# Both halves of a split input as one moving operand, and a reciprocal in pieces

## The chip, the cores and the metric

The kernel runs on one core of a Trainium2 chip. The metric is the device time of one execution in microseconds (us). TensorE multiplies 128x128 weight tiles (the stationary operand) with a moving operand of 256 or 512 columns here, into banks of PSUM (128x512 fp32 each); VectorE (DVE), ScalarE (ACT) and GpSimd (POOL) do the rest, and each works off its own queue of instructions in order. SyncE (SP) issues most of the DMAs.

## The reference

One layer of a streaming encoder over 256 frames of 2048 features. Four mixers share one input projection, each has a gate as wide as the model, and a SwiGLU block follows:

```python
h = rms_norm(x, norm_mix_pre[l])
z = h @ w_in[l]
z_conv, z_gla, z_diff, z_rwkv, z_gate = jnp.split(z, _offsets(TOP_SIZES), axis=-1)
...
merged = gates[:, :, 0] * (o_conv @ w_branch[l, 0])
...
# gla: log_a = log_sigmoid(w_lr @ w_a2 + b_a) / GLA_LOGIT_NORM
```

The sum over the four gated branches goes through `w_out`, a second norm and a residual, and then through gate, up and down projections of 5632 features. All products are wanted at fp32 accuracy. In the linear attention (gla), a log-sigmoid of the decay is computed with a series that needs one reciprocal of a 128x512 tile.

## The kernel before, in words

**Split products.** fp32 accuracy is built from operands rounded to fp32r. Each operand is held as a rounded half (`hi`) and the remainder (`lo`), and a product is three matmuls: hi x hi, hi x lo and lo x hi. The weights come from memory in chunks of 256 rows by 512 columns (512 KB). `Stream.chunk` loads a chunk on SP's queue, rounds it on ScalarE (the cast, L600) and takes the remainder on VectorE (the subtraction, L601); it has four buffers for raw chunks and three for each of hi and lo. The normalised input is split the same way into `hT_hi` and `hT_lo` (L361 and L362, in `split_out`), 16 k-tiles of 128 features by 256 frames.

**Two kinds of product.** A token-major product (`gemm_tok`, L661 to L663) has the input as weights and 512 weight columns as the moving operand; it takes two banks, one for each 128 frames. A feature-major product (`gemm_feat`, L692, L693, L695) has the weights as stationary operand and the 256 frames as the moving one: for each k-tile and each of four column tiles, three matmuls of 256 columns. Its four results of 128x256 lie in two banks, two to a bank. The first of them (`w_l`, called l) computes its lo x hi part one chunk later (`trail`, L679), since its weights and x arrive together at the start. `x_piece` brings x in five pieces meanwhile, and `x_norm` computes the norm.

**Order of the stages.** There are ten feature-major products: l, k, r and v of the RWKV mixer one behind the other, then c1, c2 and c0 of the conv mixer, later one for q and k of the linear attention, and two for q and k of the differential attention (`dq`, twice). Between and behind them stand token-major products: gates and branch products (`gates_and_branch`), values, `w_out`, and the feed-forward block. All use one pool of four banks (`bank()`, tag mm), handed out in turn, so a product of two banks leaves the other two to be read meanwhile.

**What reads the banks.** After a feature-major product, VectorE reads each bank once, multiplying by the norm `rB`: L857 to L859 for l, L863 for k, r, v, L878 and L882 in conv, L906 and L907, L933. In the conv mixer, L572 reads c0's banks directly.

**What sets the order.** Every instruction is placed on its engine's queue by a scheduler that plays the program through with its own estimate of times and takes, among the instructions that are ready, the one of the highest priority; on the chip each queue then runs in that fixed order. `tc.high_priority(offset=e.boost)` is the priority of the chunk stream, `e.mix` (lower) that of the RWKV mixer, whose small fp32 matmuls are threaded between the large ones. The linear attention's reciprocal is L421, in `gla_mixer`.

**Places.** `gt_tile` is a ring of three buffers, for the gates, the conv mixer's ct and cu, and at the start a table. The skew (SKEW = 320 bytes) shifts where hi and lo begin in their buffers for feature-major products.

Of the kernel before, what the change touches and what calls it, by code (L numbers as in the profile page):

```python
# [13 lines left out]
SKEW = 320  # L14
# [387 lines left out]
def gla_mixer(e, q, k, wl, v, g, wa2, out_hi, out_lo):  # L402
# [18 lines left out]
    V.reciprocal(h, h)  # L421
# [160 lines left out]
class Stream:  # L582
# [5 lines left out]
    def chunk(self, ap, w=512, into=None, skew=0):  # L588

        e, nc = self.e, self.e.nc  # L590
        with e.tc.high_priority(offset=e.boost):
            raw = self.ring.tile([128, 2, 512], F32, tag="raw", name="raw", bufs=e.nraw)
            nc.sync.dma_start(raw[:, :, :w], ap)
            if into:
                hi, lo = into
            else:
                o = skew // 4
                hi, lo = (self.ring.tile([128, 1152], F32R, tag=t, name=t, bufs=e.nhi)[:, o:o + 1024].rearrange("p (k n) -> p k n", k=2)
                          for t in ("hi", "lo"))
# [5 lines left out]
def hybrid_kernel(tc, x, xt, w_l, w_in, w_branch, w_out, w_gate, w_up, w_down, post_mix, post_ffn, wa2_d, w2_d, a2_d, g2_d, lq_d,  # L605
# [4 lines left out]
    e = Env()  # L610
# [4 lines left out]
    with ExitStack() as ctx:  # L615
# [8 lines left out]
        def bank():  # L624
            return mmp.tile([128, 512], F32, tag="mm", name="mm", bufs=4)
# [40 lines left out]
        def columns(w, g):  # L666
            return lambda kc: w[kc, g]

        def gemm_feat(src, w, tiles, banks, before=None, trail=False):

            held = []

            def remainder(kc, lo):
                for k in range(2):
                    kt = 2 * kc + k
                    for j, (o, wd) in enumerate(tiles):
                        mm(banks[j // 2][:wd, (j % 2) * 256:(j % 2) * 256 + 256], lo[:, k, o:o + wd], hT_hi[:, kt, :], start=False,  # L679
                           stop=kt == 15, skip_group_check=True)  # L680

            for kc in range(8):
                if before:
                    before(kc)
                hi, lo = stream.chunk(src(kc), w, skew=SKEW)
                for k in range(2):
                    kt = 2 * kc + k
                    for j, (o, wd) in enumerate(tiles):
                        ps = banks[j // 2][:wd, (j % 2) * 256:(j % 2) * 256 + 256]
                        first, last = kt == 0 and j % 2 == 0, kt == 15  # L690
                        cs = slice(o, o + wd)
                        mm(ps, hi[:, k, cs], hT_hi[:, kt, :], start=first, stop=False, skip_group_check=True)  # L692
                        mm(ps, hi[:, k, cs], hT_lo[:, kt, :], start=False, stop=False, skip_group_check=True)  # L693
                        if not trail:
                            mm(ps, lo[:, k, cs], hT_hi[:, kt, :], start=False, stop=last, skip_group_check=True)  # L695
                if trail:
                    if held:
                        remainder(*held.pop())
                    held.append((kc, lo))
            if held:  # L700
                remainder(*held.pop())
# [5 lines left out]
        hT_hi = hpool.tile([128, 16, 256], F32R, tag="hT_hi", name="hT_hi")  # L707
        hT_lo = hpool.tile([128, 16, 256], F32R, tag="hT_lo", name="hT_lo")
# [48 lines left out]
        with ExitStack() as mctx:  # L757
# [49 lines left out]
            two = lambda b: b.rearrange("p (f t) -> p f t", f=2)  # L807
# [4 lines left out]
            with ExitStack() as rctx:  # L812
# [33 lines left out]
                for q, c0 in (("l", None), ("k", COL["rk"]), ("r", COL["rr"]), ("v", COL["rv"])):  # L846
# [3 lines left out]
                    bk = [bank(), bank()]  # L850
                    if q == "l":
                        gemm_feat(lambda kc: w_l[kc], 464,
                                  [(0, 112), (112, 96), (208, 128), (336, 128)], bk, before=first_x, trail=True)
# [3 lines left out]
                        V.tensor_tensor(z[:96, 0:2, 1:257], two(bk[0])[:96], rb2(rB, slice(0, 96)), op=ALU.mult)  # L857
                        V.tensor_tensor(glw[96:112], bk[0][96:112, 0:256], rB[96:112], op=ALU.mult)
                        V.tensor_tensor(z[:, 2:4, 1:257], two(bk[1]), rb2(rB), op=ALU.mult)  # L859
                    else:  # L860
                        gemm_feat(columns(w_in, c0), 512, [(128 * j, 128) for j in range(4)], bk, before=then_tables(q))
                        for p in range(2):
                            V.tensor_tensor(z[:, 2 * p:2 * p + 2, 1:257], two(bk[p]), rb2(rB), op=ALU.mult)  # L863
# [10 lines left out]
                bk = [bank(), bank()]  # L874
                ctiles = [(128 * j, 128) for j in range(4)]
                gemm_feat(columns(w_in, COL["c1"]), 512, ctiles, bk)
                for p in range(2):
                    V.tensor_tensor(ct[:, 2 * p:2 * p + 2], two(bk[p]), rb2(rB2), op=ALU.mult)  # L878
                bk = [bank(), bank()]
                gemm_feat(columns(w_in, COL["c2"]), 512, ctiles, bk)  # L880
                for p in range(2):
                    V.tensor_tensor(cu[:, 2 * p:2 * p + 2, 2:258], ct[:, 2 * p:2 * p + 2], two(bk[p]), op=ALU.mult)  # L882
                bk = [bank(), bank()]
                gemm_feat(columns(w_in, COL["c0"]), 512, ctiles, bk)
                conv_mixer(e, cu, [two(b) for b in bk], rB, ct, *oT)
# [10 lines left out]
            with ExitStack() as sctx:  # L896
# [7 lines left out]
                bk = [bank(), bank()]  # L904
                gemm_feat(columns(w_in, COL["gqk"]), 512, ctiles, bk)
                V.scalar_tensor_tensor(q, two(bk[0]), 0.125, rb2(rB), op0=ALU.mult, op1=ALU.mult)  # L906
# [291 lines left out]
```

## Time and profile before

| | |
|---|---|
| median of 3 runs | 1647.31 us (1645.69 to 1647.57) |
| the profiled execution's own time | 1645.97 us |
| its span, first to last instruction | 1644.2 us |
| instructions | 21813, of which 8632 matmuls |
| read from HBM | 302.40 MB, 186 GB/s over the span |

The profile is of one execution. The span is shorter than the time of the execution by what lies around it. A matmul's busy time (281 ns for 256 columns, 390 for 512) overlaps the next one's, so a mean duration is not the pace at which they follow each other; the distance of two starts is. PEld is the loading of weights, which runs beside the matmuls.

### The profile page before, as it was taken

The numbers are of one execution on the slowest core, as the hardware profiler recorded it, in microseconds if no ns is written. First come the engines' busy times: TensorE is split into PE (matmuls) and PEld (weight loads), VectorE is DVE, ScalarE is ACT, GpSimd is POOL, SyncE is SP. The second block draws the span as 40 slices with busy tenths as digits, with TensorE's granted clock in tenths as the row PEclk, the third lists the DMA queues.
The fourth block names the chain that finished last, engine by engine and source line by source line (L and its number), as shares of the span: only waits on it lengthen the run. The fifth ranks groups of instructions, "written<-read, shape, count | busy, mean of one in ns | idle before, by whom it ended". The sixth has DMA issues, their size and how long they took to land.

```text
span 1644.2 us, 21813 instructions
## 1 busy us (share of the span) xinstructions
PE 1630.3 (99%) x8632; PEld 1384.2 (84%) x8632; DVE 994.8 (61%) x1176; ACT 759.6 (46%) x879; POOL 33.1 (2%) x46
## 2 busy tenths in 40 slices
PE   9999999999999999999999999999999999999997
PEld 9999988887789978888888888888888888888886
DVE  7568784669764477455655655444544555556555
ACT  6353443346554355444444644444444444445443
POOL 0000110000000001000000000000000000000000
PEclk9999999999999999999999999999999999999999
DMA  8554565345556545765555565555555555555563
GB/s 297 181 168 149 180 213 178 130 143 165 171 164 196 187 158 184 269 192 184 190 192 196 191 191 190 186 189 191 191 187 189 188 193 191 190 194 191 193 194 139
DMA packets 86118, 306.84 MB, mean 187 GB/s; under 512 B 9600, under 2 KB 12176, under 8 KB 85504
## 3 DMA queue, kind: packets, MB, share of 16 engines
q1 hardware_dynamic: 84352, 298.85, 55.6%
q0 software_dynamic: 1232, 5.95, 1.2%
q8 instruction: 67, 1.10, 0.3%
q10 hardware_dynamic: 432, 0.66, 0.2%
q14 instruction: 35, 0.29, 0.1%
HBM read 302.40 MB, written 3.01 MB: 186 GB/s over the span
## 4 chain that ended last, share of the span: by engine, by line
PE 97%; issue 1%; ACT 1%; DVE 1%; DMA 0%; POOL 0%; DVEq 0%; POOLq 0%; ACTq 0%
PE mm L662 22%; PE mm L663 21%; PE mm L661 21%; PE mm L692 5%; PE mm L693 4%; PE mm L695 4%; PE mm L1075 2%; PE mm L1077 2%; PE mm L1076 2%; PE wd L1077 2%; PE wd L1076 2%; PE wd L1075 2%; PE tq L1053 1%; PE mm L679 0%; PE ps L465 0%
## 5 line engine op out<-in xcount | busy, mean ns | idle before, releaser
L601 DVE TENSOR_TENSOR lo<-raw,hi 128x1024 fp32r<-128x1024 f32 (+1 forms) x554 | 676.6, 1222 | 550.9 <-ACT hi L600 548.7
L600 ACT CAST hi<-raw 128x1024 fp32r<-128x1024 f32 (+1 forms) x554 | 582.4, 1051 | 721.4 <-PE mm L663 510.1
L662 PE MATMUL mm<-lo,h_hi 128*128 128x512 f32 x704 | 274.9, 390 | 0.0
L663 PE MATMUL mm<-hi,h_lo 128*128 128x512 f32 x704 | 273.9, 390 | 0.1
L661 PE MATMUL mm<-hi,h_hi 128*128 128x512 f32 x704 | 250.6, 391 | 0.2 <-ACT h_hi L361 0.2
L662 PE MATMUL mm<-lo,hT_hi 128*128 128x512 f32 x608 | 238.8, 393 | 2.3 <-DVE lo L601 2.3
L663 PE MATMUL mm<-hi,hT_lo 128*128 128x512 f32 x608 | 237.5, 391 | 0.0
L661 PE MATMUL mm<-hi,hT_hi 128*128 128x512 f32 x608 | 219.5, 391 | 0.0
L692 PE MATMUL mm<-hT_hi,hi 128*128 128x256 f32 (+2 forms) x640 | 178.8, 284 | 0.3 <-ACT hi L600 0.3
L693 PE MATMUL mm<-hT_lo,hi 128*128 128x256 f32 (+2 forms) x640 | 177.1, 281 | 0.3 <-DVE hT_lo L362 0.3
L695 PE MATMUL mm<-hT_hi,lo 128*128 128x256 f32 x576 | 161.6, 282 | 0.0
L661 PEld LDWEIGHTS mm<-hi,h_hi 128*128 128x128 f32 x704 | 132.2, 188 | 27.8 <-ACT h_hi L361 0.9
L663 PEld LDWEIGHTS mm<-hi,h_lo 128*128 128x128 f32 x704 | 132.2, 188 | 27.6 <-DVE s L643 0.5
L662 PEld LDWEIGHTS mm<-lo,h_hi 128*128 128x128 f32 x704 | 132.2, 188 | 27.0
L662 PEld LDWEIGHTS mm<-lo,hT_hi 128*128 128x128 f32 x608 | 114.2, 188 | 27.2 <-DVE lo L601 2.7
L661 PEld LDWEIGHTS mm<-hi,hT_hi 128*128 128x128 f32 x608 | 114.1, 188 | 24.1
L663 PEld LDWEIGHTS mm<-hi,hT_lo 128*128 128x128 f32 x608 | 114.2, 188 | 23.6 <-issue 0.3
L692 PEld LDWEIGHTS mm<-hT_hi,hi 128*128 128x128 f32 (+2 forms) x640 | 119.8, 187 | 2.1 <-ACT hi L600 0.8
L693 PEld LDWEIGHTS mm<-hT_lo,hi 128*128 128x128 f32 (+2 forms) x640 | 120.1, 188 | 1.4 <-DVE hT_lo L362 0.5
L695 PEld LDWEIGHTS mm<-hT_hi,lo 128*128 128x128 f32 x576 | 108.7, 189 | 0.6
L1077 PE MATMUL mm<-hi,al 128*128 128x512 f32 x168 | 65.4, 389 | 0.0
L1076 PE MATMUL mm<-lo,ah 128*128 128x512 f32 x168 | 65.4, 389 | 0.0
(367 smaller groups left out, 1688.3 us busy)
## 6 DMA issues: line engine op xcount, KB each, us to landing
raw<-in_w_in_dram SPq DMA_DIRECT2D x224, 512.0 KB, 3.5
raw<-in_w_gate_dram SPq DMA_DIRECT2D x88, 512.0 KB, 3.5
raw<-in_w_up_dram SPq DMA_DIRECT2D x88, 512.0 KB, 3.5
raw<-in_w_down_dram SPq DMA_DIRECT2D x88, 512.0 KB, 3.5
raw<-in_w_branch_dram SPq DMA_DIRECT2D x32, 512.0 KB, 4.0
raw<-in_w_out_dram SPq DMA_DIRECT2D x32, 512.0 KB, 3.5
raw<-in_w_l_dram SPq DMA_DIRECT2D x8, 464.0 KB, 7.3
xs<-in_x_dram POOLq DMA_DIRECT2D x1, 2048.0 KB, 12.2
```

Source lines behind the costliest of these rows:

```text
L600: nc.scalar.copy(hi[:, :, :w], raw[:, :, :w])
L601: nc.vector.tensor_tensor(lo[:, :, :w], raw[:, :, :w], hi[:, :, :w].bitcast(F32), op=ALU.subtract)
L661: mm(banks[i_], ah[:, ts], hi[:, k, :], start=kt == 0, stop=False)
L662: mm(banks[i_], ah[:, ts], lo[:, k, :], start=False, stop=False)
L663: mm(banks[i_], al[:, ts], hi[:, k, :], start=False, stop=kt == nk - 1)
L692: mm(ps, hi[:, k, cs], hT_hi[:, kt, :], start=first, stop=False, skip_group_check=True)
L693: mm(ps, hi[:, k, cs], hT_lo[:, kt, :], start=False, stop=False, skip_group_check=True)
L695: mm(ps, lo[:, k, cs], hT_hi[:, kt, :], start=False, stop=last, skip_group_check=True)
L1053: T.transpose(ps[:, k, i * 128:(i + 1) * 128], sg[:, i, (2 * kp + k) * 128:(2 * kp + k + 1) * 128], ident)
L1075: mm(bk[j][i], ah[:, k, ts], hi[:, k, :], start=kt == 0, stop=False)
L1076: mm(bk[j][i], ah[:, k, ts], lo[:, k, :], start=False, stop=False)
L1077: mm(bk[j][i], al[:, k, ts], hi[:, k, :], start=False, stop=kt == 43)
```

## The change

The two halves of the input are laid side by side in one tile `hT`, per k-tile 256 columns of hi and 256 of lo, so that hi-weights x both is one matmul of 512 columns into a whole bank; lo-weights x hi, 256 columns, adds onto the first half of the bank. Each column tile has a bank of its own, so a feature-major product takes all four. At its end, `take` copies the bank's second half to the destination on ScalarE and adds the first half to it on VectorE, both at the stream's priority; the multiplication by the norm follows as a separate step in SBUF. In the first and the last chunk of a product the column tiles are computed one behind the other, in other chunks k-tile by k-tile. The skew is 0 for hi and 64 bytes for lo. The conv mixer has a further buffer `cb` from the ring. The reciprocal is four of 128x128. The tiles that later take hT's place (`h2`, `wl`) become one tile each.

```diff
     V.tensor_scalar(h, x, 2.0, None, op0=ALU.add)
-    V.reciprocal(h, h)
+    for j in range(2):
+        for p in range(2):
+
+            V.reciprocal(h[:, j, p * 128:(p + 1) * 128], h[:, j, p * 128:(p + 1) * 128])
     V.tensor_tensor(x, x, h, op=ALU.mult)
...
-                o = skew // 4
-                hi, lo = (self.ring.tile([128, 1152], F32R, tag=t, name=t, bufs=e.nhi)[:, o:o + 1024].rearrange("p (k n) -> p k n", k=2)
-                          for t in ("hi", "lo"))
+                hi, lo = (self.ring.tile([128, 1152], F32R, tag=t, name=t, bufs=e.nhi)[:, o // 4:o // 4 + 1024].rearrange("p (k n) -> p k n", k=2)
+                          for t, o in zip(("hi", "lo"), skew))
...
-        def gemm_feat(src, w, tiles, banks, before=None, trail=False):
+        def gemm_feat(src, w, tiles, before=None, trail=False):
+
 
 
 
             held = []
-
-            def remainder(kc, lo):
-                for k in range(2):
-                    kt = 2 * kc + k
-                    for j, (o, wd) in enumerate(tiles):
-                        mm(banks[j // 2][:wd, (j % 2) * 256:(j % 2) * 256 + 256], lo[:, k, o:o + wd], hT_hi[:, kt, :], start=False,
-                           stop=kt == 15, skip_group_check=True)
+            bk = [bank() for _ in tiles]
+
+            def rounded(kc, hi, k, j):
+                o, wd = tiles[j]
+                mm(bk[j][:wd], hi[:, k, o:o + wd], hT[:, 2 * kc + k].rearrange("p a t -> p (a t)"), start=kc == k == 0, stop=False,
+                   skip_group_check=True)
+
+            def remainder(kc, lo, k, j):
+                o, wd = tiles[j]
+                mm(bk[j][:wd, 0:256], lo[:, k, o:o + wd], hT_hi[:, 2 * kc + k, :], start=False, stop=kc == 7 and k == 1,
+                   skip_group_check=True)
+
+            def order(kc):
+                kj = [(k, j) for k in range(2) for j in range(len(tiles))]
+
+                return sorted(kj, key=lambda x: x[1]) if kc in (0, 7) else kj
 
             for kc in range(8):
                 if before:
                     before(kc)
-                hi, lo = stream.chunk(src(kc), w, skew=SKEW)
-                for k in range(2):
-                    kt = 2 * kc + k
-                    for j, (o, wd) in enumerate(tiles):
-                        ps = banks[j // 2][:wd, (j % 2) * 256:(j % 2) * 256 + 256]
-                        first, last = kt == 0 and j % 2 == 0, kt == 15
-                        cs = slice(o, o + wd)
-                        mm(ps, hi[:, k, cs], hT_hi[:, kt, :], start=first, stop=False, skip_group_check=True)
-                        mm(ps, hi[:, k, cs], hT_lo[:, kt, :], start=False, stop=False, skip_group_check=True)
-                        if not trail:
-                            mm(ps, lo[:, k, cs], hT_hi[:, kt, :], start=False, stop=last, skip_group_check=True)
+                hi, lo = stream.chunk(src(kc), w, skew=(0, 64))
+                for k, j in order(kc):
+                    rounded(kc, hi, k, j)
+                    if not trail:
+                        remainder(kc, lo, k, j)
                 if trail:
-                    if held:
-                        remainder(*held.pop())
                     held.append((kc, lo))
-            if held:
-                remainder(*held.pop())
+                    for c, l in held if kc == 7 else held[:-1]:
+                        for k, j in order(c):
+                            remainder(c, l, k, j)
+                    held = held[-1:]
+
+            def take(dst, j, r=slice(0, 128)):
+                with tc.high_priority(offset=e.boost):
+                    S.copy(dst, bk[j][r, 256:512])
+                    V.tensor_tensor(dst, dst, bk[j][r, 0:256], op=ALU.add)
+            return take
 
         def lhs_h(kt):
             return hT_hi[:, kt, :], hT_lo[:, kt, :]
 
 
-        hT_hi = hpool.tile([128, 16, 256], F32R, tag="hT_hi", name="hT_hi")
-        hT_lo = hpool.tile([128, 16, 256], F32R, tag="hT_lo", name="hT_lo")
+        hT = hpool.tile([128, 16, 2, 256], F32R, tag="hT", name="hT")
+        hT_hi, hT_lo = hT[:, :, 0], hT[:, :, 1]
...
                     if q == "l":
-                        gemm_feat(lambda kc: w_l[kc], 464,
-                                  [(0, 112), (112, 96), (208, 128), (336, 128)], bk, before=first_x, trail=True)
+                        take = gemm_feat(lambda kc: w_l[kc], 464,
+                                         [(0, 112), (112, 96), (208, 128), (336, 128)], before=first_x, trail=True)
+                        for j in range(4):
+                            p = slice(0, 96 if j < 2 else 128)
+                            take(z[p, j, 1:257], j, p)
+                            if j == 0:
+                                take(glw[96:112], 0, slice(96, 112))
                         x_norm()
                         o = VCOL["w0"][0]
                         V.tensor_scalar(half, vec[:, o:o + 8], 0.5, None, op0=ALU.mult)
-                        V.tensor_tensor(z[:96, 0:2, 1:257], two(bk[0])[:96], rb2(rB, slice(0, 96)), op=ALU.mult)
-                        V.tensor_tensor(glw[96:112], bk[0][96:112, 0:256], rB[96:112], op=ALU.mult)
-                        V.tensor_tensor(z[:, 2:4, 1:257], two(bk[1]), rb2(rB), op=ALU.mult)
+                        V.tensor_tensor(z[:96, 0:2, 1:257], z[:96, 0:2, 1:257], rb2(rB, slice(0, 96)), op=ALU.mult)
+                        V.tensor_tensor(glw[96:112], glw[96:112], rB[96:112], op=ALU.mult)
+                        V.tensor_tensor(z[:, 2:4, 1:257], z[:, 2:4, 1:257], rb2(rB), op=ALU.mult)
                     else:
-                        gemm_feat(columns(w_in, c0), 512, [(128 * j, 128) for j in range(4)], bk, before=then_tables(q))
-                        for p in range(2):
-                            V.tensor_tensor(z[:, 2 * p:2 * p + 2, 1:257], two(bk[p]), rb2(rB), op=ALU.mult)
+                        take = gemm_feat(columns(w_in, c0), 512, ctiles, before=then_tables(q))
+                        for j in range(4):
+                            take(z[:, j, 1:257], j)
+                        V.tensor_tensor(z[:, :, 1:257], z[:, :, 1:257], rb4(rB), op=ALU.mult)
...
-                bk = [bank(), bank()]
-                ctiles = [(128 * j, 128) for j in range(4)]
-                gemm_feat(columns(w_in, COL["c1"]), 512, ctiles, bk)
-                for p in range(2):
-                    V.tensor_tensor(ct[:, 2 * p:2 * p + 2], two(bk[p]), rb2(rB2), op=ALU.mult)
-                bk = [bank(), bank()]
-                gemm_feat(columns(w_in, COL["c2"]), 512, ctiles, bk)
-                for p in range(2):
-                    V.tensor_tensor(cu[:, 2 * p:2 * p + 2, 2:258], ct[:, 2 * p:2 * p + 2], two(bk[p]), op=ALU.mult)
-                bk = [bank(), bank()]
-                gemm_feat(columns(w_in, COL["c0"]), 512, ctiles, bk)
-                conv_mixer(e, cu, [two(b) for b in bk], rB, ct, *oT)
+                cb = gt_tile()[:, 0:1024].rearrange("p (f t) -> p f t", f=4)
+                take = gemm_feat(columns(w_in, COL["c1"]), 512, ctiles)
+                for j in range(4):
+                    take(ct[:, j], j)
+                V.tensor_tensor(ct, ct, rb4(rB2), op=ALU.mult)
+                take = gemm_feat(columns(w_in, COL["c2"]), 512, ctiles)
+                for j in range(4):
+                    take(cu[:, j, 2:258], j)
+                V.tensor_tensor(cu[:, :, 2:258], cu[:, :, 2:258], ct, op=ALU.mult)
+                take = gemm_feat(columns(w_in, COL["c0"]), 512, ctiles)
+                for j in range(4):
+                    take(cb[:, j], j)
+                conv_mixer(e, cu, [cb[:, 0:2], cb[:, 2:4]], rB, ct, *oT)
...
-                bk = [bank(), bank()]
-                gemm_feat(columns(w_in, COL["gqk"]), 512, ctiles, bk)
-                V.scalar_tensor_tensor(q, two(bk[0]), 0.125, rb2(rB), op0=ALU.mult, op1=ALU.mult)
-                V.tensor_tensor(k, two(bk[1]), rb2(rB), op=ALU.mult)
+                take = gemm_feat(columns(w_in, COL["gqk"]), 512, ctiles)
+                for j in range(4):
+                    take((q, k)[j // 2][:, j % 2], j)
+                V.scalar_tensor_tensor(q, q, 0.125, rb2(rB), op0=ALU.mult, op1=ALU.mult)
+                V.tensor_tensor(k, k, rb2(rB), op=ALU.mult)
...
-                    bk = [bank(), bank()]
-                    gemm_feat(columns(w_in, COL["dq"] + c), 512, ctiles, bk)
-                    for p in range(2):
-                        V.scalar_tensor_tensor(t[:, 2 * p:2 * p + 2], two(bk[p]), 0.125 if c == 0 else 1.0, rb2(rB), op0=ALU.mult, op1=ALU.mult)
+                    take = gemm_feat(columns(w_in, COL["dq"] + c), 512, ctiles)
+                    for j in range(4):
+                        take(t[:, j], j)
+                    V.scalar_tensor_tensor(t, t, 0.125 if c == 0 else 1.0, rb4(rB), op0=ALU.mult, op1=ALU.mult)
...
-            h2_hi = hpool.tile([128, 16, 256], F32R, tag="hT_hi", name="h2_hi")
-            h2_lo = hpool.tile([128, 16, 256], F32R, tag="hT_lo", name="h2_lo")
+            h2 = hpool.tile([128, 2, 16, 256], F32R, tag="hT", name="h2")
+            h2_hi, h2_lo = h2[:, 0], h2[:, 1]
```

## Rows read from the trace of the kernel before

**Rows 1.** The page: busy us, share and instructions of each engine.
```profile
PE 1630.3 (99%) x8632; PEld 1384.2 (84%) x8632; DVE 994.8 (61%) x1176; ACT 759.6 (46%) x879; POOL 33.1 (2%) x46
```

**Rows 2.** The page: the chain that ended last, shares by engine.
```profile
PE 97%; issue 1%; ACT 1%; DVE 1%; DMA 0%; POOL 0%; DVEq 0%; POOLq 0%; ACTq 0%
```

**Rows 3.** The page's costliest groups: feature-major matmuls; count, busy us, mean ns, idle before.
```profile
L692 PE MATMUL mm<-hT_hi,hi 128*128 128x256 f32 (+2 forms) x640 | 178.8, 284 | 0.3 <-ACT hi L600 0.3
L693 PE MATMUL mm<-hT_lo,hi 128*128 128x256 f32 (+2 forms) x640 | 177.1, 281 | 0.3 <-DVE hT_lo L362 0.3
...
L695 PE MATMUL mm<-hT_hi,lo 128*128 128x256 f32 x576 | 161.6, 282 | 0.0
```

**Rows 4.** Windows: us, busy us by engine (instructions), granted clock, DMA share, GB/s.
```profile
58.14:66.62 8.48, 8.48 (x74) 8.48 (x73) 5.71 (x8) 3.14 (x3) 0.00 (x0) 1.00 0.57 186
134.41:142.57 8.16, 8.16 (x75) 8.16 (x73) 8.16 (x13) 3.16 (x3) 0.00 (x0) 1.00 0.44 140
538.31:560.92 22.61, 22.61 (x194) 22.61 (x193) 11.11 (x11) 8.39 (x8) 0.00 (x0) 1.00 0.56 187
800.00:808.16 8.16, 8.16 (x37) 6.76 (x36) 3.67 (x3) 3.65 (x4) 0.00 (x0) 1.00 0.58 191
```

**Rows 5.** Timeline around the reciprocal: start, us, engine, line, what [idle before <-releaser].
```profile
370.56 1.05 ACT L600 CAST hi<-raw 128x1024 fp32r<-128x1024 f32 x1
...
372.17 3.34 DVE L421 RECIPROCAL h<-h 128x512 f32<-128x512 f32 x1
...
373.73 0.61 PE L661 MATMUL mm<-hi,hT_hi 128*128 128x512 f32 x2
...
375.43 2.29 DVE L601 TENSOR_TENSOR lo<-raw,hi 128x1024 fp32r<-128x1024 f32 x2
...
376.64 0.50 PE L662 MATMUL mm<-lo,hT_hi 128*128 128x512 f32 x1 [2.29 <-DVE lo L601]
```

**Rows 6.** Timeline at the end of the second feature-major product, k.
```profile
52.57 1.05 ACT L600 CAST hi<-raw 128x1024 fp32r<-128x1024 f32 x1 [1.78 <-PE mm L693]
...
53.65 1.23 DVE L601 TENSOR_TENSOR lo<-raw,hi 128x1024 fp32r<-128x1024 f32 x1 [1.60 <-ACT hi L600]
...
55.08 0.28 PE L693 MATMUL mm<-hT_lo,hi 128*128 128x256 f32 x1
...
55.32 0.28 PE L692 MATMUL mm<-hT_hi,hi 128*128 128x256 f32 x1
...
55.40 1.05 ACT L600 CAST hi<-raw 128x1024 fp32r<-128x1024 f32 x1 [1.78 <-PE mm L693]
...
56.31 1.23 DVE L107 TENSOR_TENSOR zm_k<-Z 128x1024 f32<-128x1024 f32 x1
```

**Rows 7.** Lines L132 and L109: duration ns min/median/max, first and last start.
```profile
L132 ACT COPY Gt<-ps x4: 372/376/388, 118.6 to 123.3; 128x256 f32<-128x256 f32 x4
L109 DVE SCALAR_TENSOR_TENSOR zm_k<-zm_k,vec,Z x4: 480/482/485, 58.6 to 59.8; 128x256 f32<-128x256 f32 x4
```

**Rows 8.** Timeline at the end of the first feature-major product, l.
```profile
31.24 2.36 DVE L601 TENSOR_TENSOR lo<-raw,hi 128x1024 fp32r<-128x1024 f32 x2 [0.53 <-issue]
...
31.94 0.28 PE L692 MATMUL mm<-hT_hi,hi 128*128 128x256 f32 x1
```

**Rows 9.** Timeline at the start of the first feature-major product.
```profile
6.96 0.70 PE L692 MATMUL mm<-hT_hi,hi 128*112 128x256 f32 x2
...
7.46 1.67 DVE L362 SCALAR_TENSOR_TENSOR hT_lo<-acc,vec,hT_hi 128x256 fp32r<-128x256 f32 x4
...
8.00 0.37 PE L693 MATMUL mm<-hT_lo,hi 128*112 128x256 f32 x1 [0.33 <-DVE hT_lo L362]
...
13.27 0.37 PE L692 MATMUL mm<-hT_hi,hi 128*112 128x256 f32 x1 [0.33 <-ACT hi L600]
```

**Rows 10.** Lines L575 and L791: duration ns min/median/max, first and last start.
```profile
L575 DVE TENSOR_TENSOR oT<-gt,oT x1: 1208/1208/1208, 193.8 to 193.8; 128x1024 fp32r<-128x1024 f32 x1
L791 ACT ACTIVATE gt<-mm,rst x32: 678/687/692, 208.2 to 808.4; 128x512 f32<-128x512 f32 x32
```

More of the change, by code (lines that the diff above doesn't have):

```diff
@@ L13 @@
 PSUM = bass.MemoryType.PSUM
-SKEW = 320
 VCOL = {}
@@ L586, in __init__, with chunk @@
         self.e, self.ring = e, ring
-    def chunk(self, ap, w=512, into=None, skew=0):
+    def chunk(self, ap, w=512, into=None, skew=(0, 0)):
         e, nc = self.e, self.e.nc
@@ L805, in gates_and_branch @@
                         done(g)
-            two = lambda b: b.rearrange("p (f t) -> p f t", f=2)
+            ctiles = [(128 * j, 128) for j in range(4)]
+            rb4 = lambda t: t.unsqueeze(1).to_broadcast([128, 4, 256])
             lev32 = gt_tile()[:, 0:768].rearrange("p (l t) -> p l t", l=6)
@@ L929, in hybrid_kernel @@
                     t = e.M.tile([128, 4, 256], F32, tag="m4", name="qk")
-                    bk = [bank(), bank()]
-                    gemm_feat(columns(w_in, COL["dq"] + c), 512, ctiles, bk)
-                    for p in range(2):
-                        V.scalar_tensor_tensor(t[:, 2 * p:2 * p + 2], two(bk[p]), 0.125 if c == 0 else 1.0, rb2(rB), op0=ALU.mult, op1=ALU.mult)
+                    take = gemm_feat(columns(w_in, COL["dq"] + c), 512, ctiles)
+                    for j in range(4):
+                        take(t[:, j], j)
+                    V.scalar_tensor_tensor(t, t, 0.125 if c == 0 else 1.0, rb4(rB), op0=ALU.mult, op1=ALU.mult)
                     qk.append(t)
@@ L1086, in hybrid_kernel @@
                 if hf == 1:
-                    wide = [hpool.tile([128, 16, 256], F32R, tag=t, name="wl").rearrange("p (c k x) n -> p c k (x n)", c=4, k=2)
-                            for t in ("hT_hi", "hT_lo")]
+                    wide = hpool.tile([128, 2, 16, 256], F32R, tag="hT", name="wl")
+                    wide = [wide[:, t].rearrange("p (c k x) n -> p c k (x n)", c=4, k=2) for t in range(2)]
                     al_, ch_ = {}, {}
```

## The prediction

> **What bounds the kernel now.** I read the busy shares first: TensorE is busy 1630.3 of 1644.2 us [rows 1]. The chain of waits agrees: 97% of the span is TensorE [rows 2]. So only three things can move the end: the pace at which matmuls start, a TensorE stall that goes, and a new one that comes. The ten feature-major products (`gemm_feat`) are 640 matmuls on L692, 640 on L693, 576 on L695 and, in the first product, 64 on L679: 1920 in all [rows 3]; a chunk of weights is 24 of them, a product 8 chunks. Their busy times overlap, so the pace is read from windows that begin and end at a matmul's start. Two paces are seen [rows 4]: three chunks (72 matmuls) took 8.48 us, 117.8 ns each, and a whole product took 22.61 us for 192, again 117.8; but three other chunks took 8.16 us, 113.3 ns each. Matmuls of 512 columns took 8.16 us for 36, 226.7 ns each: exactly twice the quick pace. The granted clock is 1.00 in all four windows, so the difference is none of the clock's. Reading the starts of all 80 chunks, about 54 are at the slow pace (6 of the first product, 5 of the second, 32 of the four that no mixer's matmuls cut into, 11 of the other four), the rest at the quick one or waiting for input.
>
> **The change part by part.** *512 columns.* For each of 640 pairs of k-tile and column tile, three matmuls of 256 columns become one of 512 and one of 256. The columns are the same; 640 starts go. A slow chunk now takes 24 x 117.8 = 2.827 us; at twice the quick pace, 8 x (226.7 + 113.3) = 2.720. At best 54 x 0.107 = 5.8 us go. No row shows a 256 between two 512s. If each remaining 256 keeps the slow pace (+4.45 ns x 640 = 2.85 us), the gain is 2.9. If a 512 beside moving hT is slowed by twice that 4.45, a pair takes 226.7 + 8.9 + 117.8 = 353.4 ns = 3 x 117.8: gain 0 in the slow chunks. I take 4.4, midway between the first two, since every row of a 512 has 226.7 and only the 256 is open; ends 0 and 5.8.
>
> The Trainium skill, TensorE: Matmul & The Clock Gate, section Back-to-back issue gap, has a start-to-start of N/2.4 + 2.5 ns: a fixed 2.5 ns per matmul. By it the 640 removed starts would give 1.6 us instead of 4.4 and the sum -1.2 (an estimate). The rows differ: 2 x 113.3 = 226.7 leaves no fixed part, and at the slow pace a pair of 256s costs 8.9 ns over one 512 [rows 4].
>
> *The reciprocal.* It holds VectorE 3.34 us; the cast before the first queued lo was done at 371.61 (370.56 + 1.05), but that lo began at 375.43, and TensorE stood 2.29 us [rows 5]: two matmuls of 0.227 from 373.73, next due 374.19, started 376.64, so 2.45 us lost. In four pieces of 0.84 us a lo can go in after the first (373.01 + 1.22 = 374.23, on time). What is late next is the second lo, due a chunk later and so covered. But VectorE runs in program order: if the scheduler queues all four pieces ahead of the lo, nothing is gained. I take 2.3; ends 0 and 2.45.
>
> *Banks.* Before, a product took two of four banks and the next product the other two, so the reading of a bank had a whole product to hide under. Now each product takes four, and the next one's first matmul on bank j waits for `take(j)`: a ScalarE copy (0.376, the nearest row) and a VectorE add from PSUM (0.48) [rows 7]. In the first and last chunk the tiles are in turn, each 2 x (0.227 + 0.113) = 0.68 us, so every bank has about 3 x 0.68 = 2.04 us between its last matmul and the next product's first on it. A quiet path needs about 0.2 + 0.4 + 0.5 and fits. What is queued around it is read at the second product's end, T = 55.32 [rows 6]. A cast starts 2.75 us before T and one 0.08 after it, 0.32 after the matmul that frees its buffer (55.08); lo subtractions follow, one from T - 1.67 to T - 0.44. Bank 0: its copy ends about T - 1.3, its add waits for that lo and ends near T + 0.0: 0.1 late. Bank 3: its buffer's cast is released one matmul before its copy is, so the copy starts at about T + 1.05 and ends at 1.47; by then the next lo (T + 1.18, 1.22 long) may be running, so the add ends at 2.8, against 2.04 wanted: 0.75 late; with the add first, on time. If a mixer operation of 1.23 [rows 6] stands in front too, 1.9 late. Six boundaries between feature products: I take 0.2 each, 1.2 us, near the quiet order; ends 0 and 6 x 1.9 = 11.4. Where a token-major product follows (three times) it needs banks 0 and 1 first: 0.1 in all. Where one stands ahead, two of the banks have long been free.
>
> The first product ends on another order: its remainders come last, eight matmuls of 256, so bank 0 has only 6 x 0.118 = 0.7 us. Its copy ends at about T (31.94), two lo's hold VectorE from 31.24 for 2.36 us [rows 8], and bank 0 has a second part (`glw`) to copy and add. With one lo first: add from 32.4, both adds done 33.3, 1.4 us late; with none in the way 0.7, with both 2.6. I take 1.4.
>
> *Start.* The first matmul now needs both halves of hT at once: it starts at 8.00 rather than 6.96. Its second tile's lower half comes at about 8.4, then seven more of 0.227: the chunk ends at 10.0, not 9.8. That is hidden: TensorE waits for a cast until 13.27 anyway [rows 9]. Cost 0; without that cover, 0.2.
>
> *Elsewhere.* Each product adds about 1.6 us of adds to VectorE and 1.5 of copies to ScalarE, 16 and 15 in ten products. Both have idle time (61% and 46% busy) [rows 1]. The conv mixer gets one more multiplication and its y shares a buffer with the first gate; its last step starts at 193.8, 14 us before that gate's first sigmoid at 208.2 [rows 10]. No DMA moves, and the same bytes come in.
>
> **Sum.** -4.4 - 2.3 + 1.2 + 0.1 + 1.4 = -4.0 us. The profiled execution took 1645.97 us (1.77 around its span), so 1642.0 there; the median of the runs is 1.34 above it, so 1643.3.
>
> **Rivals.** (1) *The banks queue.* The adds stand behind a lo and a mixer operation at all six boundaries: 11.4 + 2.6 + 0.1 - 4.4 - 2.3 = +7.4, 1654.7; it decides from 0.67 us per boundary on, where 2.6 + 0.1 + 6 x 0.67 equals the 6.7 gained; from 1.2 on it shows. For: VectorE is 67% busy there (5.71 of 8.48 us, [rows 4]) and keeps its queue's order; against: the reads are short and each has 2.04 us. Chance 0.18. (2) *The pace doesn't move*: -2.3 + 2.7 = +0.4, 1647.7. For: nothing shows what sets the slow pace; against: no 512 row shows it. 0.17. (3) *All goes well*: -5.8 - 2.45 + 0.7 = -7.5, 1639.8. For: the quick pace appears within the same products; 0.16. (4) *A start is worth little*: a removed start saves something, but less than the 2.9 us in which the remaining 256s keep the slow pace; midway to the 0 of rival 2 that is 1.4: -1.4 - 2.3 + 2.7 = -1.0, 1646.3. For: at the quick pace two 256s cost no more than a 512; against: 54 of 80 chunks are not at that pace. 0.07. The page's fixed part, above, falls here.
>
> **How the numbers follow.** My forecast has 0.42, with its own range 1641 to 1647. About 0.2% (3.3 us) is what a measurement can tell. Faster than 1644.0: 0.27 of my 0.42, rival 3's 0.16, 0.05 of the rest: 0.48. Slower than 1650.6: 0.13 of rival 1 and 0.04 of the rest: 0.17. Within: 0.35. The range, 1639.5 to 1650.5, takes in rival 3 and leaves out the worse part of rival 1.
>
> **What would show it.** Pace: a chunk of a feature product without mixer matmuls at 2.72 to 2.76 us (2.83 means rival 2). Reciprocal: four VectorE pieces of some 0.84 us with a lo among them and no TensorE idle near 374. Banks: TensorE's idle before the first matmul of a column tile, released by VectorE's add; about 0.2 us each as I say, over 0.67 by rival 1. I am wrong if TensorE's new idle adds up to more than 5 us, or if lo's elsewhere come late because adds and copies went ahead of them.

## The result, and the profile after

The changed kernel takes 1657.99 us (median of 4 runs, 1657.10 to 1660.01) against 1646.61 for the kernel before (4 runs beside it): ratio 1.0071, 95% interval 1.0059 to 1.0084. It is slower, and 7.5 us above the end of the range. The kernel before has two groups of times over all its executions, 1645.6 to 1646.7 us and 1647.2 to 1648.1 us, at mean granted clocks of 0.998 and mostly 0.997, so a median of few executions can differ from another by 1.6 us by chance. The profiled executions stand at 1657.10 and 1645.97 us, spans 1655.3 and 1644.2. From the page of the changed kernel: busy line, the chain's shares, and the two feature-major groups (they answer [rows 1 to 3]).

```profile
PE 1632.8 (99%) x7992; PEld 1356.9 (82%) x7992; DVE 1010.6 (61%) x1213; ACT 769.4 (46%) x918; POOL 33.6 (2%) x46
...
PE 96%; DVE 2%; ACT 1%; issue 1%; DMA 0%; POOL 0%; DVEq 0%; POOLq 0%; ACTq 0%
...
L680 PE MATMUL mm<-hT,hi 128*128 128x512 f32 (+2 forms) x640 | 213.7, 398 | 2.7 <-DVE Z L711 1.5
L685 PE MATMUL mm<-hT,lo 128*128 128x256 f32 (+2 forms) x640 | 159.1, 283 | 0.0
```

The 640 starts are gone (7992 matmuls, not 8632), and VectorE has 2% of the chain where it had 1%. The page does not say where 11 us went. The starts of TensorE's stages in the two timelines do:

| first matmul of | before, us | after, us | after - before |
|---|---|---|---|
| l | 6.96 | 7.96 | +1.00 |
| k | 31.94 | 34.33 | +2.39 |
| c1 | 100.54 | 102.35 | +1.81 |
| gqk (linear attention's q and k) | 308.74 | 311.33 | +2.59 |
| the first half of gv (gv0) | 342.89 | 357.30 | +14.41 |
| second differential-attention product (dq1) | 538.31 | 549.82 | +11.51 |
| the first gate after it (g1.0) | 584.64 | 595.56 | +10.92 |
| the last matmul | 1634.41 | 1645.33 | +10.92 |

All of the loss lies in one step: from gqk to gv0, +11.82 us. The rest nets to -0.9: the end of l +2.39, three products k, r, v -0.58, the conv mixer with its gates +0.78, gv0 to dq1 -2.90 (TensorE's 2.29 us of idle at the reciprocal are absent, and 24 of the mixer's small matmuls have run before gv0 already), dq1 and the product of values behind it -0.59. The changed kernel's timeline where gqk ends (start, us, engine, line, what, idle before it and releaser):

```profile
343.74 0.28 PE L685 MATMUL mm<-hT,lo 128*128 128x256 f32 x1
...
346.94 1.15 PE L305 MATMUL ps<-W,AM 128*64 128x64 f32 x16 [1.27 <-DVE W L303]
348.01 2.07 PE L412 MATMUL ps<-glw,wa 16*128 16x256 f32 x4
354.53 0.68 PE L340 MATMUL psl<-ident,X 64*128 64x64 f32 x4 [4.45 <-DVE X L338]
...
355.30 0.65 ACT L710 COPY q<-mm 128x256 f32<-128x256 f32 x2 [4.24 <-PE psl L340]
...
356.83 0.74 DVE L711 TENSOR_TENSOR q<-q,mm 128x256 f32<-128x256 f32 x2
...
357.30 0.80 PE L662 MATMUL mm<-hi,hT 128*128 128x512 f32 x1 [2.08 <-DVE q L711]
```

gqk's last matmul starts at 343.74, but ScalarE's first `take` of it only at 355.30. It waited for the last transposes of the RWKV mixer (L340), not for TensorE's product. `q` and `k` are tiles of the linear-attention mixer's pool S1, opened in the code where RWKV's pool R closes. While they wait, gqk's result fills all four banks, so gv0 has none. TensorE is left with the mixer's last matmuls, which wait on one another through VectorE, ScalarE and GpSimd, and then with the copies and adds: 1.27 + 4.45 + 2.08 = 7.80 us idle.

The kernel before reads gqk late too, and it cost nothing there. Its timeline, TensorE's first gv0 matmul and VectorE's read of gqk:

```profile
342.89 0.40 PE L661 MATMUL mm<-hi,hT_hi 128*128 128x512 f32 x1
...
363.51 0.68 DVE L906 SCALAR_TENSOR_TENSOR q<-mm,rB 128x512 f32<-128x512 f32 x1
```

gqk is read 20.6 us after it ended, but it holds two banks, and gv0 runs on the other two, with the mixer's matmuls between its own. The clock adds to it; windows of the changed kernel (us, busy us by engine with instructions, granted clock, DMA share, GB/s):

```profile
349.00:357.00 8.00, 1.77 (x7) 0.83 (x5) 4.55 (x11) 2.30 (x6) 1.63 (x1) 0.50 0.01 3
...
358.00:362.00 4.00, 4.00 (x12) 3.10 (x11) 3.70 (x7) 3.31 (x4) 0.00 (x0) 0.54 0.00 0
362.00:370.00 8.00, 8.00 (x37) 6.46 (x36) 7.95 (x10) 3.18 (x4) 0.00 (x0) 1.00 0.13 29
```

The granted clock is 0.50, the 1.2 GHz level, in the idle stretch and some 4.4 us into gv0: ten matmuls of 512 columns start 0.43 us apart instead of 0.227, about 2 us. It had fallen at about 348 (1.00 in the window 347 to 348, 0.52 in 348 to 349), ahead of the longest idle stretch, when TensorE had been idle for 1.27 us and had otherwise run the mixer's small matmuls.

The pace, and three smaller places. First the window of dq1, a whole product (it answers the 22.61 of [rows 4]); then the start of l (answers [rows 9]), the end of l (answers [rows 8]), the end of k (answers [rows 6]), and the reciprocal (answers [rows 5]):

```profile
549.82:572.17 22.35, 22.35 (x131) 19.59 (x129) 12.17 (x14) 9.48 (x12) 0.00 (x0) 1.00 0.57 189
```

```profile
7.96 1.43 PE L680 MATMUL mm<-hT,hi 128*112 128x512 f32 x5 [0.78 <-DVE hT L361]
...
13.24 0.95 PE L680 MATMUL mm<-hT,hi 128*112 128x512 f32 x3 [0.38 <-ACT hi L601]
...
32.26 0.22 DVE L763 COPY rr<-rst 128x128 f32<-128x128 f32 x1
32.40 0.41 DVE L711 TENSOR_TENSOR Z<-Z,mm 96x256 f32<-96x256 f32 x1
32.54 0.33 PE L764 MATMUL ps<-ident,rr 128*128 128x128 f32 x1 [0.46 <-DVE rr L763]
32.73 1.21 DVE L602 TENSOR_TENSOR lo<-raw,hi 128x1024 fp32r<-128x1024 f32 x1
33.87 1.07 DVE L711 TENSOR_TENSOR Z<-Z,mm 96x256 f32<-96x256 f32 x3
34.33 0.50 PE L680 MATMUL mm<-hT,hi 128*128 128x512 f32 x1 [1.47 <-DVE Z L711]
...
57.64 0.50 PE L680 MATMUL mm<-hT,hi 128*128 128x512 f32 x1
...
363.53 3.38 DVE L423 RECIPROCAL h<-h 128x128 f32<-128x128 f32 x4
```

Four reciprocal pieces stand back to back with no lo among them; the lo follows at 366.83. At the end of k the first 512 lasts 0.50 us instead of 0.39; the first chunk of a product takes 2.88 us where its others take 2.77 to 2.79, so a boundary costs 0.11 (0.23 at the end of k; in the conv mixer the first chunks of c2 and c0 take 2.97 and 3.02). At the end of l the adds are split by a lo, the order that the prediction priced at 1.4 to 2.6.

### The profile page after: what moved, and what is told of

Same layout as the page of the kernel before. It is cut to its first block, busy times and chain, and to the rows that moved or that the text cites. A ratio compares the mean times of both kernels' runs of the same rounds, so it can differ in the third digit from the quotient of the medians.

```text
span 1655.3 us, 20621 instructions
## 1 busy us (share of the span) xinstructions
PE 1632.8 (99%) x7992; PEld 1356.9 (82%) x7992; DVE 1010.6 (61%) x1213; ACT 769.4 (46%) x918; POOL 33.6 (2%) x46
## 4 chain that ended last, share of the span: by engine, by line
PE 96%; DVE 2%; ACT 1%; issue 1%; DMA 0%; POOL 0%; DVEq 0%; POOLq 0%; ACTq 0%
PE mm L662 22%; PE mm L663 22%; PE mm L664 22%; PE mm L680 8%; PE mm L685 4%; PE mm L1094 2%; PE mm L1095 2%; PE mm L1096 2%; PE wd L1095 2%; PE wd L1096 2%; PE wd L1094 2%; PE tq L1072 1%; PE ps L467 0%; DVE lo L602 0%; ACT hT L360 0%
## 5 line engine op out<-in xcount | busy, mean ns | idle before, releaser
L663 PE MATMUL mm<-lo,h 128*128 128x512 f32 x704 | 274.9, 390 | 0.0
L664 PE MATMUL mm<-hi,h 128*128 128x512 f32 x704 | 273.9, 390 | 0.1
L662 PE MATMUL mm<-hi,h 128*128 128x512 f32 x704 | 250.6, 391 | 0.2 <-ACT h L360 0.2
L663 PE MATMUL mm<-lo,hT 128*128 128x512 f32 x608 | 239.4, 394 | 0.0
L664 PE MATMUL mm<-hi,hT 128*128 128x512 f32 x608 | 238.1, 392 | 0.0
L662 PE MATMUL mm<-hi,hT 128*128 128x512 f32 x608 | 221.1, 393 | 2.1 <-DVE q L711 2.1
L680 PE MATMUL mm<-hT,hi 128*128 128x512 f32 (+2 forms) x640 | 213.7, 398 | 2.7 <-DVE Z L711 1.5
L685 PE MATMUL mm<-hT,lo 128*128 128x256 f32 (+2 forms) x640 | 159.1, 283 | 0.0
L662 PEld LDWEIGHTS mm<-hi,h 128*128 128x128 f32 x704 | 132.2, 188 | 27.8 <-ACT h L360 0.9
L664 PEld LDWEIGHTS mm<-hi,h 128*128 128x128 f32 x704 | 132.2, 188 | 27.6 <-DVE s L644 0.5
L663 PEld LDWEIGHTS mm<-lo,h 128*128 128x128 f32 x704 | 132.2, 188 | 27.0
L680 PEld LDWEIGHTS mm<-hT,hi 128*128 128x128 f32 (+2 forms) x640 | 117.2, 187 | 28.2 <-DVE Z L711 2.2
L662 PEld LDWEIGHTS mm<-hi,hT 128*128 128x128 f32 x608 | 114.5, 189 | 26.3 <-DVE q L711 2.3
L664 PEld LDWEIGHTS mm<-hi,hT 128*128 128x128 f32 x608 | 114.6, 189 | 24.0 <-issue 0.3
```

What stands on the lines that cost most here:

```text
L662: mm(banks[i_], ah[:, ts], hi[:, k, :], start=kt == 0, stop=False)
L663: mm(banks[i_], ah[:, ts], lo[:, k, :], start=False, stop=False)
L664: mm(banks[i_], al[:, ts], hi[:, k, :], start=False, stop=kt == nk - 1)
L680: mm(bk[j][:wd], hi[:, k, o:o + wd], hT[:, 2 * kc + k].rearrange("p a t -> p (a t)"), start=kc == k == 0, stop=False, skip_group_check=True)
L685: mm(bk[j][:wd, 0:256], lo[:, k, o:o + wd], hT_hi[:, 2 * kc + k, :], start=False, stop=kc == 7 and k == 1, skip_group_check=True)
```

## The experiments

**e1, the wait of gqk.** The result is taken into a tile of another pool (`gt`, free by then) and multiplied into `q` and `k` when these come free. What waits is then a multiplication, not the emptying of a bank.

```
+ cq = gt_tile()[:, 0:1024].rearrange("p (f t) -> p f t", f=4)
- take((q, k)[j // 2][:, j % 2], j)
+ take(cq[:, j], j)
- V.scalar_tensor_tensor(q, q, 0.125, rb2(rB), ...)
+ V.scalar_tensor_tensor(q, cq[:, 0:2], 0.125, rb2(rB), ...)   # k likewise, from cq[:, 2:4]
```

> The changed kernel with one edit: the gla q/k product is taken into a free gate buffer (gt ring) and only multiplied from there into q and k. Theory A: q and k lie in a pool that opens in the RWKV mixer's space, so their first write waits for the whole mixer; as the product now holds all four banks, the next product waits too. Then TensorE's idle between 345 and 357 us goes, the half clock behind it goes, the step of 11.8 us at the start of gv0 shrinks to under 1, and the time is 1645 to 1649. Rival B: the copies and adds made the RWKV chain itself late; then TensorE waits for its transposes wherever the results go, and the time stays above 1654.

1648.27 us, ratio to before 1.0008 (0.9999 to 1.0017): the loss is gone. The step from gqk to gv0 is -1.6 instead of +11.82 (with 116 of the mixer's small matmuls in it, where the kernel before has 136, so the -1.6 is no gain of its own). Theory A's range was met. The timeline of e1:

```profile
342.15 0.65 ACT L710 COPY gt<-mm 128x256 f32<-128x256 f32 x2
...
345.56 0.28 PE L685 MATMUL mm<-hT,lo 128*128 128x256 f32 x1
345.68 0.40 PE L662 MATMUL mm<-hi,hT 128*128 128x512 f32 x1
```

gv0's first matmul follows gqk's last at once, though the RWKV mixer is still at work.

**e2, gqk alone.** The kernel after with all other products in the old form (two banks, 256 columns) and the reciprocal whole: only gqk takes four banks.

> The other way round: all products in the old form (two banks, 256 columns, skew 320, reciprocal whole), the gla q/k product alone in the new form with its results written straight into q and k. Theory A: this one edit costs most of the loss, 8 to 13 us over the kernel before, 1655 to 1660, with TensorE idle ahead of gv0. Rival B: without the other nine products' copies and adds nothing is late, at most 1.5 us over, 1646 to 1648.

1655.70 us, ratio 1.0058 (1.0045 to 1.0072), as theory A says; gv0 starts 11.79 us later than before. TensorE and ScalarE wait as in the whole change:

```profile
351.92 0.69 PE L340 MATMUL psl<-ident,X 64*128 64x64 f32 x4 [4.45 <-DVE X L338]
...
352.69 0.65 ACT L707 COPY q<-mm 128x256 f32<-128x256 f32 x2 [4.24 <-PE psl L340]
...
354.68 0.80 PE L659 MATMUL mm<-hi,hT 128*128 128x512 f32 x1 [2.08 <-DVE q L708]
```

One of ten products makes the whole step of 11.8 us. The step is there though the other nine products have their old form (e2), and gone though they have the new one (e1): the two show the cause from both sides.

**e3, the reciprocal alone.** The kernel before with the four pieces and nothing else.

> The kernel before with the reciprocal in four pieces and nothing else. As predicted: a lo slips in behind the first piece, the idle of 2.3 us on TensorE goes, -2.3 us, about 1644.3. Theory C: the four pieces stand one behind the other in VectorE's queue, ahead of the three lo's, as in the changed kernel; then the idle stays and the time is within 0.7 us of before, 1646 to 1647.3.

1647.47 us, ratio 1.0002 (0.9993 to 1.0011). VectorE's queue and TensorE's stall in e3:

```profile
372.18 3.38 DVE L421 RECIPROCAL h<-h 128x128 f32<-128x128 f32 x4
375.47 3.43 DVE L601 TENSOR_TENSOR lo<-raw,hi 128x1024 fp32r<-128x1024 f32 x3
...
376.69 0.50 PE L662 MATMUL mm<-lo,hT_hi 128*128 128x512 f32 x1 [2.33 <-DVE lo L601]
```

All four pieces were queued ahead of the lo: 2.33 us of stall, against 2.29 in [rows 5]. Theory C was right. Smaller pieces help only where another instruction is queued between them: in e1 and e4 a lo stands behind the third piece, and TensorE is idle for 0.94 us there.

**e4, l in the old form.** e1, with the first product again on two banks and 256 columns.

```
- take = gemm_feat(lambda kc: w_l[kc], 464, [...], before=first_x, trail=True)
...
+ bk = [bank(), bank()]
+ old_feat(lambda kc: w_l[kc], 464, [...], bk, before=first_x, trail=True)
...
```

> As the first run, and the first product l back in its old form (256 columns, two banks, read late). If the waits at the end of l (0.6 and 1.7 us of idle) come from the emptying of its four banks, the second product starts 2.0 to 2.6 us earlier and the time is 2 to 2.6 under the first run, 1643 to 1646.5. Rival: TensorE waits there for the norm's transposes anyway; then within 0.7 of the first run.

1644.46 us, ratio 0.9986 (0.9977 to 0.9995), 3.8 under the median of e1, more than the 2 to 2.6 expected. k now starts while both lo's of that stretch still hold VectorE (e4's timeline), since the other two banks are free:

```profile
31.07 2.36 DVE L602 TENSOR_TENSOR lo<-raw,hi 128x1024 fp32r<-128x1024 f32 x2 [0.54 <-issue]
31.76 0.39 PE L680 MATMUL mm<-hT,hi 128*128 128x512 f32 x1
```

In e1 k began 2.86 us later than in e4 (34.62 against 31.76), somewhat more than the 2.39 of the kernel after. The product k then took 1.54 us longer, which is e1's own: the granted clock was 0.83 behind that wait, where the kernel after, with the same wait, has 1.00 (window 37 to 42 us, first e1, then after):

```profile
37.00:42.00 5.00, 5.00 (x26) 4.33 (x25) 3.98 (x9) 0.78 (x2) 0.00 (x0) 0.83 0.29 117
```

```profile
37.00:42.00 5.00, 5.00 (x31) 4.40 (x30) 4.70 (x9) 2.39 (x3) 0.00 (x0) 1.00 0.20 79
```

This accounts for the excess. Three of e1's ten executions took 1646.6 to 1646.9 us at a mean granted clock of 0.998 or more, seven 1648.2 to 1648.7 at 0.997, the profiled one among them; e4 lies some 2.3 under the three, as expected. So the emptying of l's banks costs about 2.3 us, and in most executions of e1 another 1.5; in the profiled one that is the clock.

**e6 and e7, where the weights lie.** The change also moved the remainder's tile within its buffer: rounded part and remainder began 320 bytes in, and now begin at 0 and 64. e6 is e4 with both at 320, e7 with both at 0.

```
- hi, lo = stream.chunk(src(kc), w, skew=(0, 64))
+ hi, lo = stream.chunk(src(kc), w, skew=(320, 320))     # e7: (0, 0)
```

> The fourth run (e4) with hi and lo shifted by 320 bytes each in the nine new products, as all products had before. Theory D: the pace of a chunk (2.774 to 2.787 us against 2.720 at the quick pace) comes from where the weights lie; then it moves by 0.03 or more per chunk, 2 to 4 us in the 72 chunks, either way. Theory E: it comes from the alternation of 512 and 256 columns; then chunks stay at 2.77 to 2.79 and the time within 0.8 us of e4's 1644.5.

> The same with no shift at all. D: another pace again, 2 to 4 us; E: chunks at 2.77 to 2.79, within 0.8 us of 1644.5.

e6 1646.36 us, ratio 0.9996 (0.9987 to 1.0005); e7 1645.73, 0.9993 (0.9983 to 1.0002); e4 had 1644.46, and the three groups of times do not overlap. At 1.9 and 1.3 us above e4 they lie between theory E's 0.8 and D's 2 to 4. Place matters: the window of dq1 in e4, then in e6:

```profile
536.89:559.28 22.39, 22.39 (x131) 19.63 (x129) 12.17 (x14) 9.48 (x12) 0.00 (x0) 1.00 0.55 188
```

```profile
538.51:561.07 22.56, 22.56 (x131) 19.57 (x129) 12.18 (x14) 9.48 (x12) 0.00 (x0) 1.00 0.56 186
```

e7 took 22.56 us for it too, but 22.41 for r, where e4 has 22.36 and e6 22.55.

**e8, the order of the first and last chunk.** e4 without the sorting by column tile in them.

> e4 with the column tiles k-tile by k-tile in the first and last chunk too. Each bank then has 3 x 0.35 = 1.04 us between its last matmul and the next product's first on it, not 2.04. By the reckoning of the prediction (bank 3's add ends 2.8 us after the product's end, or 1.9 with the add first) each of the five boundaries between new products waits 0.9 to 1.8 us: 4 to 9 us slower, 1648 to 1654. Rival: the reads are quick enough that the order doesn't matter, within 0.8 us of 1644.5.

1644.62 us, ratio 0.9986 (0.9976 to 0.9995), like e4; the first chunk of dq1 takes 2.88 us without the sorting too, and the 4 to 9 us of the prediction's reckoning are not there. On the sorting rested the prediction's 2.04 us between two uses of a bank; it buys nothing here.

**e9, 512 columns alone.** e4 without the matmuls of the remainder in the nine new products (their output lacks that part); a single execution.

> e4 without the lo x hi matmuls of the nine new products (the remainder of the weights is left out of the computation), so that only 512-column matmuls beside hT are left there. If a 512 beside hT has the same pace as elsewhere, the starts in such a chunk lie 226.7 ns apart and the extra of a chunk comes from the alternation; if 230 to 231 as in the changed kernel, it is hT as the moving operand that costs 3 to 4 ns each. Time some 9 x 64 x 0.117 = 67 us shorter where the weights keep up, less where TensorE then waits for the casts.

1614.12 us. Six chunks of eight matmuls of 512 columns (window of e9, in the first dq product): 10.88 us for 48, 226.7 ns each.

```profile
492.21:503.09 10.88, 10.88 (x50) 9.01 (x48) 8.57 (x10) 6.23 (x6) 0.00 (x0) 1.00 0.70 223
```

So hT as a moving operand doesn't by itself slow a 512. Beside 256s, in after and e4, the same 512s start on average 230 to 232 ns before the next matmul, the 256s 115 to 118 (means of single chunks of dq0 and dq1).

e9 also shows rival 1's wait at work. Its products have a third fewer columns, and at seven of their ends TensorE stands idle for 1.13 to 4.53 us until one of VectorE's adds is done; behind dq0:

```profile
508.00 1.20 PE L680 MATMUL mm<-hT,hi 128*128 128x512 f32 x4 [1.13 <-DVE qk L709]
```

**e10, the place alone.** The kernel before, with the remainder's tile at 64 and the rounded part's at 0.

> The kernel before, unchanged but for one thing that the change also did: the remainder's tile begins 64 bytes further into its buffer than the rounded part's, instead of both 320 bytes in. Operands stay 256 columns wide, a product stays in two banks. Theory E (the place of the weights sets the pace, the 512 columns give little): chunks of feature products fall from 2.83 to at most 2.78 us, the time by 2 to 4 us. Theory F (only the merged columns help): chunks stay at 2.72 to 2.83 and the time within 1 us of before.

1649.78 us, ratio 1.0016 (1.0007 to 1.0024): slower. Windows of e10, dq1 and the stretch that answers the quick 8.16 of [rows 4]:

```profile
540.70:563.32 22.62, 22.62 (x195) 22.62 (x194) 11.12 (x11) 8.42 (x8) 0.00 (x0) 1.00 0.57 187
134.91:143.41 8.50, 8.50 (x74) 8.50 (x73) 8.50 (x14) 3.16 (x3) 0.00 (x0) 1.00 0.46 137
```

The slow pace stays and the quick one is lost; neither theory expected that. Neither half of the gain comes alone: for dq1, 22.61 before, 512 columns at the old place give 22.56, the new place with 256 columns 22.62, both together 22.39.

**e11, the remainders of a chunk behind its 512s.** e4; in the middle six chunks all eight matmuls of 512 come first, then all eight of 256.

```
- for k, j in order(kc):
-     rounded(kc, hi, k, j)
...
-     remainder(kc, lo, k, j)
...
+ for k, j in order(kc):       # middle six chunks
+     rounded(kc, hi, k, j)
+ for k, j in order(kc):
+     remainder(kc, lo, k, j)
...
```

> e4 with each of the middle six chunks of a feature product in another order: first its eight matmuls of 512 columns, then its eight of 256, instead of in turn. Theory G (it is the turn from 256 to 512 and back that costs, since 512s alone start every 226.7 ns): a chunk takes 2.72 to 2.74 us instead of 2.78, and the nine new products give 1.5 to 2.5 us. Theory H (the remainder's weights or hT's place cost it whatever the order): 2.77 to 2.79 and no change.

1642.46 us, ratio 0.9973 (0.9962 to 0.9983): faster than both kernels and than e4, but not for theory G's reason. The pace hardly moves (dq1 22.30 against 22.39, a middle chunk 2.78 as before): theory G is refuted. Eight 512s behind one another in dq1 take 1.84 us, 229.8 ns each, though only the first and the last of them have a 256 next to them (window of e11):

```profile
543.83:545.67 1.84, 1.84 (x10) 1.51 (x9) 1.84 (x2) 1.51 (x2) 0.00 (x0) 1.00 0.03 9
```

What goes is TensorE's idle time: in e4 it was idle for 0.35 us before 157.31 and for 0.94 before 381.06, in e11 at neither place. That is 1.29 of the 2.0 us between the two medians; the rest is not traced. At the reciprocal e4 needs a lo that stands behind three pieces; in e11 one more lo was done ahead of them (timelines of e4, then e11):

```profile
377.36 2.57 DVE L423 RECIPROCAL h<-h 128x128 f32<-128x128 f32 x3
379.85 1.16 DVE L602 TENSOR_TENSOR lo<-raw,hi 128x1024 fp32r<-128x1024 f32 x1
...
381.06 0.50 PE L663 MATMUL mm<-lo,hT 128*128 128x512 f32 x1 [0.94 <-DVE lo L602]
```

```profile
379.00 1.22 DVE L602 TENSOR_TENSOR lo<-raw,hi 128x1024 fp32r<-128x1024 f32 x1 [0.51 <-ACT hi L601]
...
380.48 3.38 DVE L423 RECIPROCAL h<-h 128x128 f32<-128x128 f32 x4
383.77 2.29 DVE L602 TENSOR_TENSOR lo<-raw,hi 128x1024 fp32r<-128x1024 f32 x2
...
384.99 0.50 PE L663 MATMUL mm<-lo,hT 128*128 128x512 f32 x1
```

**e12, the same in token-major products.** e11, with the four remainder matmuls of a lone chunk behind its eight others.

> e11 with the token-major products in the same manner: in each chunk of weights that runs by itself, first the eight matmuls with the rounded part, then the four with the remainder, so that a remainder is wanted some 1.8 us later. If the stall that the reciprocal leaves (1.1 us in e4 near 380) is only a remainder that comes late, it goes, and the time falls by about 1.1 us against e11; a rival: the next remainder behind the reciprocal's pieces comes late instead, and nothing is gained.

1642.93 us, ratio 0.9976 (0.9967 to 0.9986), 0.5 above e11: the stall it was to remove was gone in e11 already, so it doesn't tell the two expectations apart.

## Why the prediction was wrong, point by point

*The step that failed* is in the part on banks: "Where a token-major product follows (three times) it needs banks 0 and 1 first: 0.1 in all." One of the three took 11.8 us. The prediction worked out when ScalarE and VectorE could read a bank, from their durations and queues. It took for granted that what they write, `q` and `k`, was free. The rows to look for stood in the trace of before: VectorE's read of gqk at 363.51, 20.6 us after the product, with nothing wrong there, because nothing needed the two banks. That slack became the wait as soon as gv0 needed them. e1 and e2 show it.

*Rival 1* (banks queue, 1654.7) has the right sign and the wrong place. It had adds behind lo's and mixer operations at six boundaries between feature products, over 0.67 us each; their first chunks show 0.1 to 0.25 (0.2 taken). It decided nothing. That its term came out near 0.2 is partly luck: by the same reckoning the sorted order was needed, and e8 does as well without it. The mechanism exists, as e9 shows, but not at this kernel's pace.

*End of l:* 1.4 taken, 2.39 measured, near the upper end given (2.6). A transpose of `rr` waits on VectorE too, and a lo stands between the adds; e4 takes it away. That such a wait can cost another 1.5 us through the clock (e1) was in no term.

*512 columns:* 4.4 taken. Of the two open ways the prediction chose the place between; measured are chunks of 2.773 to 2.787 us where a slow one had 2.827. Over a whole product dq1 fell from 22.61 to 22.35, boundary included. 54 slow chunks gain some 0.05 us each, 2.7; the chunks that had the quick pace, at 2.720, lose about as much, and up to 26 of them make 1.4: about 1.3 net (an estimate from these chunks). The starts of e4's stages say less. From k to the first gate it takes 154.76 us, 0.35 of idle included, against 154.58 before, with as many of the mixer's matmuls. From gqk to dq0 it takes 1.27 less, no more than the 1.35 by which the reciprocal's idle is shorter, and dq0 and dq1 together take 44.60 against 45.23. So the term gave some 0.4 to 0.8 us where 4.4 was taken. Two things were missed: the quick pace was itself at stake, and the weights' new place, which the prediction left out altogether, is needed for the gain: without it dq1 gets 0.05 us shorter instead of 0.22 (e6), and by itself it gains nothing (e10).

*Reciprocal:* 2.3 taken, 0 in e3. The caveat was there ("if the scheduler queues all four pieces ahead of the lo, nothing is gained") and was what happened. In e1 and e4 a lo stands behind the third piece, and 0.94 of the 2.29 us of idle is left. The kernel after has no stall there, but its pieces come 6.2 us behind gv0's first matmul, against 29.3 before, so that says nothing of the pieces.

*Right:* the start is hidden (l begins 1.00 later, the next chunk waits for its cast until 13.24, before 13.27), and the boundaries between feature products are small in this kernel. The mark set for being wrong, over 5 us of new TensorE idle, was met by 7.80 in one place.

*Open:* what in the places of weights and moving operand sets 117.8 or 113.3 ns, and why a 512 takes 226.7 ns in e9 and 229.8 in e11. The runs show that it depends on place and width together, and that the turn from one width to the other is not what costs; they do not show how.

## What to carry to other kernels

Before an operand is kept longer in PSUM, look up in the old trace when its bank was really read, and what the reader writes into: a read that comes 20 us late for nothing is a wait in store. Copy such a result into space that is free for certain, and let the multiplication into the scarce tile wait instead. Cutting a long instruction in pieces gains nothing unless the queue shows another one between them.

## What the runs showed of the hardware

The start distance of fp32r matmuls, with the granted clock at 1.00, depends on where the stationary tiles begin: the same 72 matmuls of 256 columns took 8.16 us with both tiles 320 bytes into their buffers, and 8.50 with them at 0 and 64 (before and e10). The place is not all of it, since other chunks of the kernel before take 8.48 us with both tiles at 320. Matmuls of 512 columns beside hT start 226.7 ns apart where no 256s are left in the products (e9), and 229.8 apart in rows of eight where they are (e11).

Like waits had unlike consequences for the clock. In the changed kernel the granted clock was down to 0.50 (1.2 GHz) from about 348, after 1.27 us of idle and small matmuls, to 361.7, some 4.4 us after work had resumed. Behind the wait at the end of l (1.46 us in e1, 1.47 in the kernel after) it fell in e1 and not in the kernel after. The reciprocal's stall may do the same: before, e3 and e10, idle for 2.3 us there, have two groups of times about 1.6 us apart, with mean granted clocks of 0.998 and mostly 0.997, while e4, e6, e7, e8, e11 and e12, idle for at most 0.95 us there, have one each. No trace is from an upper group of those three, so this is not shown; if it is so, that stall cost more than its 2.3 us in half of the executions.
